# A hybrid decoder layer on one NeuronCore: the MLP's down projection in seven products, with the mixed weight blocks made on GpSimd

## The chip, the core and the metric

The kernel runs on one core of one Trainium2 chip. A core has five engines that work side by side, each with an instruction queue of its own that it takes strictly in order: TensorE (PE in the profile; PEld is its weight load), VectorE (DVE), ScalarE (ACT), GpSimd (POOL) and SyncE (SP), which here issues the weight loads. The metric is the device time of one execution in microseconds.

## The reference

One decoder layer on 512 tokens of 1024 features, all in float32: a mixer with three branches, a cross-attention over 256 memory tokens, and an MLP, each with a norm before it and a residual sum after it, and a last norm. The part that matters here is the MLP:

```python
def squared_relu_mlp(h, w_up, w_down):
    return jnp.square(jax.nn.relu(h @ w_up)) @ w_down        # h: 512 x 1024, w_up: 1024 x 4096, w_down: 4096 x 1024
...
h = rmsnorm(x, norm_mlp_g[l])
x = x + squared_relu_mlp(h, w_up[l], w_down[l])
return rmsnorm(x, final_g)
```

## The kernel before

**Products in three parts.** TensorE takes fp32r operands, so every float32 operand is split into a rounded high part and a low part (ACT casts the high one, DVE subtracts it from the source for the low one), and each product is three matmuls: high by high, high by low, low by high. `parts_of` does this for weights (L111 cast on ACT, L112 subtraction on DVE; both read SBUF), `split` for activations (L223, L224).

**Weights.** `Stream` holds all weight chunks (128 x 1024, 512 KB each) in the order of the plan. `load` issues their DMAs on SP into `w_raw` buffers (RAWS of them); `pump` turns loaded chunks into `w_part` tiles (WBUFS of them, a high and a low tile for each block of 1024 columns) up to AHEAD = 2 steps further than the item that is being issued needs.

**Seven products in place of eight.** A product of two matrices that are each cut into 2 x 2 blocks needs seven block products if sums of the blocks are multiplied (A11 B11, S1 T1, S2 T2, A12 B21, S3 T3, S4 B22, A22 T4; the S are mixes of activation blocks, the T of weight blocks). Six of the gate projections and twelve pairs of the up projection's output blocks are done so by `seven`, with 84 matmuls of 256 columns each (L290). Below, such a group is called a seven. `Seven` makes its weights from two loaded chunks in four steps, s0 (B11), s1 (T1 and T3), s2 (T2 and T4) and s3 (B22 and B21), which fill seven `w_part` tiles; the mixes are made by `combo`, four DVE subtractions of 512 columns into two `w_mix` buffers (L136, L137).

**The MLP.** Four rounds of 1024 hidden features. In round 0 `first_up` makes the eight blocks of 128 features by plain products, in rounds 1 to 3 four sevens make them (q0 to q3 below). After each block comes ReLU and square on ACT and a split into `u_h` and `u_l`. Then comes the down projection of that round by `items_m` and `proj_m`: plain, with the tokens as the stationary operand, 2 column halves x 4 token tiles x 8 blocks x 3 = 192 matmuls of 512 columns, added to `x` by DVE (L836). The last half of the last round runs token tile by token tile, and `final` norms and stores each tile as it is done.

**Order.** The source gives a plan of items. The tile framework's scheduler then sets the order of the instructions on each engine when the program is built, and that order is fixed on the chip; it may move a matmul of one item between those of another.

Of the kernel before, what the change touches and what calls it, by code (L numbers as in the profile page):

```python
# [15 lines left out]
P = 128  # L16
# [16 lines left out]
UNITS, SCRS = 30, 9  # L33
RAWS, WBUFS, AHEAD = 3, 11, 2
# [4 lines left out]
def trunk_kernel(ctx: ExitStack, tc: tile.TileContext, x, mem, par, rot, dqd, kdec, g_mix, g_xa, g_mem, g_mlp,  # L39
# [40 lines left out]


# [43 lines left out]

    class Seven:

# [31 lines left out]

    class Stream:  # L160
        def __init__(self, entries):
            self.loads = [l for e in entries for l in e.loads]
            self.steps, first = [], 0
            for e in entries:
                e.first = first
                for i, st in enumerate(e.steps):
                    self.steps.append((e, st, first + (len(e.loads) if i else 1)))
# [35 lines left out]
    def run_plan():  # L203
        entries, index = [], {}
        for chunks, _ in plan:
            for kind, t, c in chunks:
                k = (t.tensor.name, c)
# [5 lines left out]
        for chunks, fn in plan:  # L213
            es = [index[(t.tensor.name, c)] for _, t, c in chunks]
# [33 lines left out]
    class Mixes:  # L248
# [27 lines left out]
        def __getitem__(self, n):  # L276
# [3 lines left out]
            return [[p[:, t0:t0 + 256] for p in self.a(k0 + k)] for k in range(4)]  # L280

    def seven(b, a):

# [10 lines left out]
        s, u, y1, y2 = scr("sv_s"), scr("sv_u"), scr("sv_1"), scr("sv_2")  # L294
# [8 lines left out]
        dve.tensor_tensor(out=y1[:, lo], in0=p2[:, lo], in1=s[:, lo], op=ALU.add)  # L303
        prod(p1, "S3", "T3", False)
        act.copy(out=u[:, hi], in_=p1[:, lo])
        dve.tensor_tensor(out=y2[:, hi], in0=s[:, hi], in1=u[:, hi], op=ALU.add)
        prod(p3, "S4", "B22", False)
        dve.tensor_tensor(out=y2[:, lo], in0=p3[:, lo], in1=u[:, lo], op=ALU.add)
        prod(p1, "A22", "T4", False)
        return y1, p1, y2  # L310
# [40 lines left out]
    def sumsq(src, c, ss, dst):  # L351

        cs = slice(c * 512, (c + 1) * 512)
        act.activation(out=dst[:, cs], in_=src[:, cs], func=AF.Square, accum_out=ss[:, c:c + 1])
# [7 lines left out]
    def norm_begin(key, src):  # L362
# [4 lines left out]
        sumsq(src, 0, ss, S["xn", key])  # L367
# [3 lines left out]
    def norm_end(key, src, g_bc):  # L371

        xn, ss = S["xn", key], S.pop(("ss", key))
        sumsq(src, 1, ss, xn)
# [593 lines left out]
    def up_done(d):  # L968
        def fn(ps):
            if d == 0:  # L970
                S["u"] = Split("u", KT)
# [179 lines left out]
```

## Time and profile before

| | |
|---|---|
| time, median of 3 runs | 1033.77 us (1033.75 to 1033.93) |
| the profiled execution | 1033.71 us; its span from first to last instruction 1032.0 us |
| PE, matmuls | 1015.5 us busy, 98% |
| DVE | 648.8 us, 63% |
| ACT | 500.7 us, 49% |
| POOL | 66.2 us, 6% |
| weight loads on SP | 27.7% of 16 DMA engines |
| mean granted TensorE clock | 0.999 |

PE's busy time counts matmuls that overlap, since one is issued while the one before still drains; how long a matmul holds PE is read from the distance between starts. The gate sevens run from about 380 to 480 us, round 0 of the MLP from about 690 to 770 us, and rounds 1 to 3 from there to the end.

### The profile page before, as it was taken

The numbers are of one execution on the slowest core, as the hardware profiler recorded it, in microseconds if no ns is written. First come the engines' busy times: TensorE is split into PE (matmuls) and PEld (weight loads), VectorE is DVE, ScalarE is ACT, GpSimd is POOL, SyncE is SP. The second block draws the span as 40 slices with busy tenths as digits, with TensorE's granted clock in tenths as the row PEclk, the third lists the DMA queues.
The fourth block names the chain that finished last, engine by engine and source line by source line (L and its number), as shares of the span: only waits on it lengthen the run. The fifth ranks groups of instructions, "written<-read, shape, count | busy, mean of one in ns | idle before, by whom it ended". The sixth has DMA issues, their size and how long they took to land.

```text
span 1032.0 us, 14325 instructions
## 1 busy us (share of the span) xinstructions
PE 1015.5 (98%) x5636; PEld 884.9 (86%) x5636; DVE 648.8 (63%) x992; ACT 500.7 (49%) x887; POOL 66.2 (6%) x118
## 2 busy tenths in 40 slices
PE   6999999999999999999999999999999999999997
PEld 4888888888888889998898888898889989989985
DVE  5567777856563796784584555466947566565643
ACT  6465567766532154463463444345416624643741
POOL 1101112321110000000100000000000000000000
PEclk9999999999999999999999999999999999999999
DMA  6322233213122212335354213223222321332222
GB/s 265 103 102 81 83 104 102 82 42 123 62 87 79 100 62 83 103 119 198 133 184 163 82 47 118 81 83 123 86 79 82 125 92 71 124 123 80 103 85 81
DMA packets 29876, 106.33 MB, mean 103 GB/s; under 512 B 3569, under 2 KB 3569, under 8 KB 29809
## 3 DMA queue, kind: packets, MB, share of 16 engines
q1 hardware_dynamic: 27216, 98.05, 27.7%
q10 hardware_dynamic: 2592, 7.37, 2.0%
q8 instruction: 44, 0.72, 0.3%
q14 instruction: 24, 0.19, 0.1%
HBM read 103.31 MB, written 2.10 MB: 102 GB/s over the span
## 4 chain that ended last, share of the span: by engine, by line
PE 97%; DMA 1%; DVE 0%; ACT 0%; SPq 0%; issue 0%; DVEq 0%; POOLq 0%; POOL 0%
PE mm L235 24%; PE mm L234 24%; PE mm L236 24%; PE p L290 17%; PE at L385 1%; PE o L546 1%; PE aT L512 1%; DMA w_raw<-in_w_in_dram 1%; PE z L488 1%; PE z L489 0%; PE xsc L236 0%; PE xsc L235 0%; PE xsc L234 0%; PE ro L693 0%; PE sc L667 0%; PE xpp L929 0%
## 5 line engine op out<-in xcount | busy, mean ns | idle before, releaser
L112 DVE TENSOR_TENSOR w_part<-w_raw,w_part 128x1024 fp32r<-128x1024 f32 (+1 forms) x180 | 210.9, 1176 | 168.1 <-PE mm L235 75.2
L111 ACT CAST w_part<-w_raw 128x1024 fp32r<-128x1024 f32 (+1 forms) x180 | 180.6, 1006 | 135.2 <-PE mm L236 79.1
L234 PE MATMUL mm<-hT_h,w_part 128*128 128x512 f32 (+1 forms) x512 | 193.6, 379 | 0.0
L235 PE MATMUL mm<-hT_l,w_part 128*128 128x512 f32 (+1 forms) x512 | 193.3, 378 | 0.0
L236 PE MATMUL mm<-hT_h,w_part 128*128 128x512 f32 (+1 forms) x512 | 193.0, 378 | 0.0
L290 PE MATMUL p<-mix_h,w_part 128*128 128x256 f32 x576 | 112.2, 283 | 0.5 <-ACT sv_s L297 0.5
L236 PEld LDWEIGHTS mm<-hT_h,w_part 128*128 128x128 f32 x512 | 96.4, 188 | 17.1
L234 PEld LDWEIGHTS mm<-hT_h,w_part 128*128 128x128 f32 x512 | 96.2, 188 | 16.8
L235 PEld LDWEIGHTS mm<-hT_l,w_part 128*128 128x128 f32 x512 | 96.5, 188 | 16.4
L235 PE MATMUL mm<-w_part,u_h 128*128 128x512 f32 x256 | 99.8, 390 | 0.0
L234 PE MATMUL mm<-w_part,u_h 128*128 128x512 f32 x256 | 98.6, 390 | 0.0
L236 PE MATMUL mm<-w_part,u_l 128*128 128x512 f32 x256 | 98.2, 389 | 0.0
L290 PEld LDWEIGHTS p<-mix_h,w_part 128*128 128x128 f32 x576 | 93.4, 192 | 1.4 <-ACT sv_s L297 0.7
L290 PE MATMUL p<-hT_h,w_part 128*128 128x256 f32 x432 | 84.4, 283 | 0.0
L290 PE MATMUL p<-mix_l,w_part 128*128 128x256 f32 x288 | 81.5, 283 | 0.0
L290 PEld LDWEIGHTS p<-hT_h,w_part 128*128 128x128 f32 x432 | 70.1, 192 | 0.8
L111 ACT CAST w_part<-w_mix 128x1024 fp32r<-128x1024 f32 x36 | 37.8, 1051 | 55.9 <-PE mm L235 37.5
L112 DVE TENSOR_TENSOR w_part<-w_mix,w_part 128x1024 fp32r<-128x1024 f32 x36 | 44.0, 1221 | 26.7 <-ACT w_part L111 20.0
L290 PE MATMUL p<-hT_l,w_part 128*128 128x256 f32 x216 | 60.7, 283 | 0.0
L236 PEld LDWEIGHTS mm<-w_part,u_l 128*128 128x128 f32 x256 | 48.1, 188 | 9.8
L235 PEld LDWEIGHTS mm<-w_part,u_h 128*128 128x128 f32 x256 | 48.1, 188 | 9.5
L234 PEld LDWEIGHTS mm<-w_part,u_h 128*128 128x128 f32 x256 | 47.9, 188 | 9.5
(211 smaller groups left out, 1813.2 us busy)
## 6 DMA issues: line engine op xcount, KB each, us to landing
w_raw<-in_w_in_dram SPq DMA_DIRECT2D x52, 512.0 KB, 3.4
w_raw<-in_w_up_dram SPq DMA_DIRECT2D x32, 512.0 KB, 3.6
w_raw<-in_w_down_dram SPq DMA_DIRECT2D x32, 512.0 KB, 3.4
w_raw<-in_w_br_dram SPq DMA_DIRECT2D x12, 512.0 KB, 3.4
w_raw<-in_w_gate_dram SPq DMA_DIRECT2D x12, 512.0 KB, 3.5
w_raw<-in_w_o_dram SPq DMA_DIRECT2D x8, 512.0 KB, 3.5
w_raw<-in_w_xk_dram SPq DMA_DIRECT2D x8, 512.0 KB, 4.2
w_raw<-in_w_xv_dram SPq DMA_DIRECT2D x8, 512.0 KB, 3.5
```

Of the source, the lines that this page charges most:

```text
L111: act.copy(out=wh, in_=src)
L112: dve.tensor_tensor(out=wl, in0=src, in1=wh.bitcast(F32), op=ALU.subtract)
L234: te.matmul(ps, lh, rh, start=first, stop=False)
L235: te.matmul(ps, lh, rl, start=False, stop=False)
L236: te.matmul(ps, ll, rh, start=False, stop=last)
L290: te.matmul(ps[:, :256], x[:, k, :], y, start=first and k == 0 and i == 0, stop=k == 3 and i == 2, skip_group_check=True)
L385: te.transpose(ps[:, k * P:(k + 1) * P], xn[:, c * P:(c + 1) * P], ident)
L488: te.matmul(z[:, :s], q[:, e, tsl], S["skh", hp][:, e, :s], start=True, stop=False)
L512: te.transpose(aps[:, sb * P:(sb + 1) * P], a[:, sb * P:(sb + 1) * P], ident)
L546: te.matmul(dst, vv, rhs, start=sb == 0 and i == 0, stop=sb == nblk and i == 1, skip_group_check=True)
```

## The change

The down projection of each round is done as seven block products as well, with the tokens as the stationary operand: for each of the seven (P1 to P7, in `ORDER`) two token tiles x 4 blocks x 3 = 24 matmuls of 512 columns, 168 a round. `_pack_d` lays the same eight chunks out by blocks: two each of B11, B12, B22, B21. `Wide` makes two blocks of 1024 columns for each product, j = 0 and 1; four of the seven (P5, P6, P7, P4) are differences of chunks and are made on GpSimd by `minus`, in place in the loaded buffers. `Seven` does its mixes with `minus` on GpSimd in place too, so that `combo` and the `w_mix` buffers go. The activations of each round are now kept as blocks: `u_ready` makes, from the squared values `s` and `u` of a pair, two sums and differences `u_v` and `u_w` in four GpSimd instructions of 256 columns, and splits `s`, `u_v`, `u_w` and half of `u` into `u_a`, `u_s`, `u_t` and `u_b`. `first_up`'s blocks 4 to 7 are done in two halves of 256 tokens. Buffers: RAWS 3 to 6, WBUFS 11 to 8, UNITS 30 to 32. The norm's statistics start from the other column half.

```diff
-UNITS, SCRS = 30, 9
-RAWS, WBUFS, AHEAD = 3, 11, 2
+UNITS, SCRS = 32, 9
+RAWS, WBUFS, AHEAD = 6, 8, 2
...
+    def minus(out, a, b):
+        pool.tensor_tensor(out=out, in0=a, in1=b, op=ALU.subtract)
...
-        def combo(self, a0, a1, b0, b1):
-            x = wpool.tile([P, CW], F32, name="w_mix", bufs=2)
-            dve.tensor_tensor(out=x[:, :512], in0=a0, in1=a1, op=ALU.subtract)
-            dve.tensor_tensor(out=x[:, 512:], in0=b0, in1=x[:, :512] if b1 is None else b1, op=ALU.subtract)
-            return x
...
         def s1(self, raw):
-            ra, rb = raw
-            self.x1 = self.combo(ra[:, 512:], ra[:, :512], rb[:, :512], ra[:, 512:])
-            return parts_of(self.x1)
+            l, r = raw[0][:, :512], raw[0][:, 512:]
+            minus(l, r, l)
+            minus(r, raw[1][:, :512], r)
+            return parts_of(raw[0])
         def s2(self, raw):
-            rb = raw[1]
-            return parts_of(self.combo(rb[:, :512], self.x1[:, :512], rb[:, 512:], None))
+            l, r = raw[0][:, :512], raw[0][:, 512:]
+            minus(l, raw[1][:, :512], l)
+            minus(r, raw[1][:, 512:], l)
+            return parts_of(raw[0])
...
+    ORDER = ("P1", "P5", "P6", "P7", "P3", "P2", "P4")
+    class Wide:
...
+            t = r["B11", j]
+            if self.p == "P1":
+                src = t
+            elif self.p == "P5":
+                minus(t, r["B12", j], t)
+                src = t
+            elif self.p == "P6":
+                minus(t, r["B22", j], t)
+                src = t
+            elif self.p == "P7":
+                src = r["B12", j]
+                minus(src, r["B22", j], src)
+            elif self.p == "P4":
+                minus(t, r["B21", j], t)
+                src = t
+            else:
+                src = r[dict(P3="B22", P2="B21")[self.p], j]
+            return parts_of(src)
...
+    def u_ready(q, s, u):
+        act.activation(out=s, in_=s, func=AF.Square)
+        act.activation(out=u, in_=u, func=AF.Square)
...
+        v, w = scr("u_v"), scr("u_w")
+        pool.tensor_tensor(out=v[:, LH], in0=u[:, RH_], in1=s[:, RH_], op=ALU.add)
+        minus(v[:, RH_], s[:, LH], u[:, RH_])
+        put("u_a", s)
+        minus(w[:, LH], v[:, LH], s[:, LH])
+        put("u_s", v)
+        minus(w[:, RH_], u[:, LH], w[:, LH])
+        hi, lo = u_parts("u_b", 0)
+        split(hi[:, q, :], lo[:, q, :], u[:, LH])
+        put("u_t", w)
...
-    for r in range(4):
-        up7(r)
-        items_m(w_down, 8 * r, lambda: S["u"], add_x(0))
-        if r < 3:
-            items_m(w_down, 8 * r + 4, lambda: S["u"], add_x(1))
...
+    LEFT = dict(P1="A11", P5="S1", P6="S2", P7="S3", P3="S4", P2="A12", P4="A22")
+    def down(r):
...
+                    for kk in range(4):
+                        ah, al = [x[:, tok] for x in u_block(LEFT[p], kk)]
+                        bh, bl = [x[:, (kk % 2) * 512:(kk % 2) * 512 + 512] for x in ws[kk // 2]]
+                        for n, (x, y) in enumerate(((ah, bh), (ah, bl), (al, bh))):
+                            te.matmul(ps, x, y, start=p in ("P1", "P5", "P2") and kk == 0 and n == 0,
+                                      stop=kk == 3 and n == 2, skip_group_check=True)
+                    t, c = TO[p]
+                    dst = S["x"][t + i][:, c * 512:(c + 1) * 512]
+                    dve.tensor_tensor(out=dst, in0=ps, in1=dst, op=ALU.add)
```

The lines move: the weight cast and subtraction are L127 and L128 in the changed kernel, the activation split L281 and L282, `minus` L143, the sevens' matmuls L349 and their copies and sums L356 to L366, the new down matmuls L1147.

**Place 1: ACT, round 2 of the MLP, around the end of seven q0.** The sevens write the PSUM tiles p1_7746 (q0) and p1_7888 (q1) before and p1_7901 and p1_8046 now. Before, w_part_7866 and w_part_7870 are the high parts of q1's s2 and s3.

```order
L297 COPY sv_s_7749<-p1_7746 128x256
L111 CAST w_part_7728<-w_raw_7627 128x1024
L111 CAST w_part_7736<-w_raw_7657 128x512
L111 CAST w_part_7742<-w_mix_7739 128x1024
L111 CAST w_part_7866<-w_mix_7863 128x1024
L299 COPY sv_s_7749<-p3_7748 128x256
L301 COPY sv_u_7750<-p1_7746 128x256
L111 CAST w_part_7870<-w_raw_7732 128x1024
```

Now w_part_8025 and w_part_8029 are the high parts of q1's s2 and s3, and L1107 is the ReLU that reads q0's last product:

```order
L360 COPY sv_u_7905<-p1_7901 128x256
L127 CAST w_part_7897<-w_raw_7693 128x1024
L1108 ACTIVATE sv_s_7904<-sv_s_7904 128x512
L1109 ACTIVATE sv_u_7905<-sv_u_7905 128x256
L1045 ACTIVATE sv_s_7904<-sv_s_7904 128x512
L281 CAST u_a_h_8005<-sv_s_7904 128x512
L1107 ACTIVATE sv_u_7905<-p1_7901 128x256
L1046 ACTIVATE sv_u_7905<-sv_u_7905 128x512
L127 CAST w_part_8025<-w_raw_7693 128x1024
L356 COPY sv_s_8049<-p1_8046 128x256
L358 COPY sv_s_8049<-p3_8048 128x256
L127 CAST w_part_8029<-w_raw_7695 128x1024
```

The cast of q1's s2 stood ahead of the copies of q0's second and third products; now it stands behind the ReLU and the square of q0's last.

**Place 2: DVE, the gate sevens, from one item to the next.** mm_3846 before and mm_3839 now are the second branch projection of an item, gt its gate; w_part_3867 before and w_part_3859 now are the low part of the next item's s2.

```order
L303 TENSOR_TENSOR sv_1_3729<-p2_3725,sv_s_3727 128x256
L308 TENSOR_TENSOR sv_2_3730<-p3_3726,sv_u_3728 128x256
L112 TENSOR_TENSOR w_part_3867<-w_mix_3863,w_part_3866 128x1024
L112 TENSOR_TENSOR w_part_3871<-w_raw_3706,w_part_3870 128x1024
L306 TENSOR_TENSOR sv_2_3730<-sv_s_3727,sv_u_3728 128x256
L112 TENSOR_TENSOR w_part_3879<-w_raw_3712,w_part_3878 128x1024
L112 TENSOR_TENSOR w_part_3884<-w_raw_3874,w_part_3884 128x512
L729 TENSOR_TENSOR gt_3844<-mm_3846,gt_3844 128x512
```

Now, with w_part_3716 the low part of the next item's s1:

```order
L787 TENSOR_TENSOR gt_3836<-mm_3839,gt_3836 128x512
L128 TENSOR_TENSOR w_part_3716<-w_raw_3540,w_part_3715 128x1024
L788 TENSOR_TENSOR mg_2563<-mg_2563,gt_3836 128x512
L787 TENSOR_TENSOR gt_3814<-mm_3817,gt_3814 128x512
L788 TENSOR_TENSOR mg_2563<-mg_2563,gt_3814 128x512
L282 TENSOR_TENSOR mgs_3833<-mg_2563,mgs_3832 128x512 x2
L128 TENSOR_TENSOR w_part_3859<-w_raw_3540,w_part_3858 128x1024
```

The next item's s1 and s2 both moved from ahead of the row that waits for the second branch projection to behind it; and s2 is now made by GpSimd in s1's buffer w_raw_3540, so that it starts only when the row of w_part_3716 is done.

**Place 3: POOL, round 2, from seven q3 to the down projection.** Before, GpSimd has no row there. Now w_raw_8033 and 8035 are B11, 8170 and 8172 B12, 8313 and 8315 B22, and u_v_8425 and u_w_8426 belong to q3:

```order
L143 TENSOR_TENSOR w_raw_8033<-w_raw_8170,w_raw_8033 128x1024
L143 TENSOR_TENSOR w_raw_8170<-w_raw_8313,w_raw_8170 128x1024
L143 TENSOR_TENSOR w_raw_8035<-w_raw_8172,w_raw_8035 128x1024
L143 TENSOR_TENSOR w_raw_8033<-w_raw_8313,w_raw_8033 128x1024
L143 TENSOR_TENSOR w_raw_8172<-w_raw_8315,w_raw_8172 128x1024
L143 TENSOR_TENSOR w_raw_8035<-w_raw_8315,w_raw_8035 128x1024
L1053 TENSOR_TENSOR u_v_8425<-sv_u_8329,sv_s_8328 128x256
L143 TENSOR_TENSOR u_v_8425<-sv_s_8328,sv_u_8329 128x256
L143 TENSOR_TENSOR u_w_8426<-u_v_8425,sv_s_8328 128x256
L143 TENSOR_TENSOR u_w_8426<-sv_u_8329,u_w_8426 128x256
```

The mixes of q3's activations stand behind six weight mixes, the last of which overwrites the buffer that P5's second block is split from.

More of the change, by code (lines that the diff above doesn't have):

```diff
@@ L158, in get, with __init__, step @@
                     for n, (i, o) in where.items()}
+    ORDER = ("P1", "P5", "P6", "P7", "P3", "P2", "P4")
+    class Wide:
+        FRESH = dict(P1=0, P5=2, P6=4, P2=6)
+        def __init__(self, t, c):
+            c0, self.p, self.raws = c
+            f = self.FRESH.get(self.p)
+            self.loads = [] if f is None else [(t, c0 + f), (t, c0 + f + 1)]
+            self.steps = [lambda raw, j=j: self.step(raw, j) for j in range(2)]
+            self.parts = []
+        def step(self, raw, j):
+            r = self.raws
+            if self.loads:
+                r[dict(P1="B11", P5="B12", P6="B22", P2="B21")[self.p], j] = raw[j]
+            t = r["B11", j]
[16 more added lines that the diff above has]
+            return parts_of(src)
+        def get(self):
+            return self.parts
     class Stream:
@@ L840, in reload_x, with proj_norm @@
         S["x"] = load_x()
-    def proj_norm(src, a, g, after):
+    def proj_norm(src, a, g, after, parts=lambda: Split("hT", KT)):
         items_m(src, 0, a, add_x(0))
@@ L1122, in _lay_out @@
         "w_up7": _pack_s(a["w_up"][0][:, U7 * P:]),
-        "w_down": np.concatenate([_pack_m(a["w_down"][0, r * D:(r + 1) * D]) for r in range(4)], axis=0),
+        "w_down": _pack_d(a["w_down"][0]),
     }
```

157 lines of the change are left out of this document (101 added, 56 removed).

## The prediction

> **What bounds the kernel now.** I read the shares of busy time, the chain that ended last, and then PE's own list of waits.
>
> ```profile
> PE 1015.5 (98%) x5636; PEld 884.9 (86%) x5636; DVE 648.8 (63%) x992; ACT 500.7 (49%) x887; POOL 66.2 (6%) x118
> ...
> PE 97%; DMA 1%; DVE 0%; ACT 0%; SPq 0%; issue 0%; DVEq 0%; POOLq 0%; POOL 0%
> ...
> PE at L385 <- DVE xn L376: 9.0, 2, 8.5
> PE p L290 <- ACT sv_s L297: 0.5, 1, 0.5
> ```
>
> PE carries 97% of the chain and waited 9.5 us in all, 8.5 of them at the start for the first norm. So the time is the number of matmuls by their distance, and any matmul taken away counts in full, as long as PE is never made to wait. The windows of the stretch that changes show the other engines' room: a stretch that is mostly sevens, and one that is mostly down projection (columns: length, then PE, PEld, DVE, ACT and POOL busy with their counts, clock, DMA).
>
> ```profile
> 843.00:890.00 47.00, 47.00 (x329) 44.18 (x328) 30.30 (x42) 23.54 (x41) 0.00 (x0) 1.00 0.21 74
> 890.00:930.00 40.00, 40.00 (x216) 34.70 (x215) 22.87 (x30) 18.15 (x30) 0.00 (x0) 1.00 0.37 126
> ...
> 843.00:890.00 47.00, 30.85 (x256) 31.02 (x257) 1.00 0.21 74
> ...
> 1016.21 0.39 PE L234 MATMUL mm<-w_part,u_h 128*128 128x512 f32 x1
> ...
> 1024.37 0.39 PE L234 MATMUL mm<-w_part,u_h 128*128 128x512 f32 x1
> ```
>
> The third row is the first window again, L290 alone: 256 matmuls of 256 columns in 30.85 us, 0.1205 us each. Between the last two rows lie 36 matmuls of 512 columns: 8.16 / 36 = 0.227 us each. GpSimd does nothing here before the change.
>
> **The matmuls, term by term.** A round of the down projection goes from 192 matmuls of 512 columns to 168; four rounds take away 96 x 0.227 = 21.8 us. `first_up`'s blocks 4 to 7 go from 96 matmuls of 512 columns to 192 of 256: 192 x 0.1205 - 21.8 = +1.3 us. Without a wait the kernel would take 1033.7 - 20.5 = 1013.2 us (the profiled execution took 1033.71, the median is 1033.77; I count from the former).
>
> **What GpSimd and DVE do to each other.** Before, GpSimd works only in the mixer. Four places where it meets DVE there (start, duration):
>
> ```profile
> 165.98 1.29 POOL L612 TENSOR_TENSOR r_sw<-r_sw,rot 128x512 f32<-128x512 f32 x1
> ...
> 166.05 1.50 DVE L500 TENSOR_TENSOR_SCAN sb_suf<-ones,sb_e 128x128 f32<-128x128 f32 x1 [0.46 <-POOL sb_e L479]
> ...
> 191.99 0.42 DVE L500 TENSOR_TENSOR_SCAN sb_suf<-ones,sb_e 128x128 f32<-128x128 f32 x1 [0.46 <-POOL sb_e L479]
> ...
> 193.47 1.30 POOL L612 TENSOR_TENSOR r_sw<-r_sw,rot 128x512 f32<-128x512 f32 x1 [1.52 <-ACT r_sw L611]
> ...
> 193.42 0.69 DVE L613 TENSOR_TENSOR r_qk<-mm,rot 128x512 f32<-128x512 f32 x1 [0.23 <-ACT r_sw L611]
> 194.15 1.70 DVE L112 TENSOR_TENSOR w_part<-w_raw,w_part 128x1024 fp32r<-128x1024 f32 x1
> ...
> 214.49 1.85 POOL L612 TENSOR_TENSOR r_sw<-r_sw,rot 128x512 f32<-128x512 f32 x1 [1.53 <-ACT r_sw L611]
> ...
> 214.02 1.22 DVE L500 TENSOR_TENSOR_SCAN sb_suf<-ones,sb_e 128x512 f32<-128x512 f32 x1
> ```
>
> A scan that takes 0.42 us took 1.50 beside a GpSimd sum and ended 0.28 us after it; L112 took 1.70 in place of 1.23, ending 1.08 us after the GpSimd sum (194.77); and the GpSimd sum of 214.49 ended 1.10 us after the scan. So an instruction of GpSimd and one of DVE with two SBUF operands run one after the other, whichever comes second waiting, while L613, whose one operand lies in PSUM, kept its 0.69. All of the weight and activation subtractions (L128, L282) have two SBUF operands; the sums from PSUM have not. I take as held: DVE 1.08 to 1.23 us for 1024 columns, GpSimd 1.10 to 1.29 for 512, and by size 2.2 to 2.6 for 1024 and 0.55 to 0.65 for 256, which no row shows. (The Trainium skill, SBUF — State Buffer, section "SBUF: two separate sides", calls this pair of ports an exclusive lock that the loser waits for through a whole instruction. The rows agree. Were it shared instead, the sevens' term below would be only the 29 us of the instruction order, and the sum 1077 us.)
>
> ```profile
> L675 POOL TENSOR_TENSOR r_qd<-r_qk,dqd x4: 1281/1298/1576, 265.2 to 319.8; 128x512 f32<-128x512 f32 x4
> ...
> L112 DVE TENSOR_TENSOR w_part<-w_raw,w_part 128x1024 fp32r<-128x1024 f32 x162 | 199.2, 1230 | 163.9 <-PE mm L235 75.2 <-issue 41.3 <-ACT w_part L111 18.9
> L224 DVE TENSOR_TENSOR u_l<-relu,u_h 128x512 fp32r<-128x512 f32 x32 | 21.8, 686 | 4.4 <-ACT u_h L223 4.4
> L729 DVE TENSOR_TENSOR gt<-mm,gt 128x512 f32<-128x512 f32 x16 | 11.0, 685 | 3.8 <-PE mm L236 3.1 <-ACT gt L773 0.7
> ...
> L111 ACT CAST w_part<-w_raw 128x1024 fp32r<-128x1024 f32 x162 | 169.6, 1049 | 108.7 <-PE mm L236 62.2 <-PE p L290 25.8 <-DMA w_raw<-in_w_in_dram 7.9
> L1011 ACT ACTIVATE relu<-relu 128x512 f32<-128x512 f32 x24 | 15.2, 638 | 0.2
> L1010 ACT ACTIVATE relu<-p 128x256 f32<-128x256 f32 x12 | 4.6, 387 | 4.3 <-PE p L290 4.1
> ```
>
> **The MLP's twelve sevens.** A seven holds PE for 84 x 0.1205 = 10.1 us. The pair of ports is held by GpSimd for four mixes (4.4 to 5.2) and four instructions of `u_ready` (2.2 to 2.6), and by DVE for the weights, 0.54 to 0.69 + 3 x 1.08 to 1.23 (3.8 to 4.4), and for the activations' low parts, three of 512 columns and one of 256 (1.9 to 2.5): 12.3 to 14.7 us. The ports, not PE, bound a seven, by 2.2 to 4.6 us. A second count goes by the order on ACT (first place shown above): q1's third product needs s2, whose cast now stands behind q0's last ReLU and square, 0.39 + 0.64 + 1.05 and then DVE's 1.23 = 3.3 us after q0's last matmul, while PE has 10 matmuls, 1.2 us, to do: 2.1 us of wait. The next block needs s3, behind it on ACT and DVE, and the one after q2's s0: about 1 us more. For q2 and q3 PE comes straight from the last matmul to a product that needs s3 (0.39 + 1.05 + 1.23 = 2.7). So some 3.2 us for three sevens in each round, 9 x 3.2 = 29 us, before any wait at the ports. Both hold at once; I take the middle of the port count, 3.4 x 12 = 41 us, and keep 26 to 55. That WBUFS falls to 8, one more than a seven fills, is why the weights can't be made a whole seven ahead as before.
>
> **The gate sevens.** Six items of 10.1 + 24 x 0.227 = 15.5 us of PE; the ports are held less than that (4.4 to 5.2, 3.8 to 4.4, one plain chunk 1.1 to 1.2, sums and splits up to 2.7: at most 13.5). But by the second place, after the second branch projection come, one behind the other, L787 0.69, s1's L128 1.23, two GpSimd mixes 2.6, s2's cast 1.05 and L128 1.23: 6.8 us, against three products or 4.3 us on PE: 2.5 us of wait, and about 0.9 more for s3, cast next. Five passages from item to item: 17 us, with 0 to 20 as ends (at 0 the sums before it run ahead).
>
> **From q3 to the down projection.** P5's second block gets its `w_part` tiles only when q3's last matmul frees them: 1.05 + 1.23 + signals = 2.4 us in which PE has nothing, and 1.1 us at P5's first block for the same reason. Behind it on POOL (third place) stand P6's second mix and q3's activations, on which P6's and P5's last matmuls wait: up to 2.5 us more. 3.5 to 6 us in each of three rounds, I take 5; in round 0, where plain products leave more time, 0 to 3, I take 2: 17 us. In the rest of a round, the ports hold 14 x 1.08 to 1.23 + 8 x 2.2 to 2.6, at most 38 us with the waits spread, in 168 x 0.227 = 38.1: covered, with no room. DMAs are the same 180 loads, and RAWS = 6 starts them sooner; nothing. Where a stage needs four chunks at once they now fill all eight `w_part` tiles, so the next stage's first weights come later by a cast and a subtraction: 0 to 5 us over four places, I take 1. ACT gains 24 weight casts and 24 splits, DVE loses 72 mixes: inside the counts above. The end, norm and store of the last tiles, stays as it is.
>
> Sum: 1033.7 - 21.8 + 1.3 + 41 + 17 + 17 + 1 = 1089 us. With the low ends (26, 0, 10, 0) 1049, with the high ones (55, 20, 21, 5) 1114.
>
> **The rivals.**
> - *PE is not kept waiting* (faster). The mixes for q0 and q1 are queued on GpSimd ahead of the down projection's end, and DVE is freed of 72 mixes of 0.69 us; if the late casts and the ports' queue were absorbed, 1013 us would come out. It decides where the waits sum to less than 20.5 us, 1.0 us for each of the 21 places (12 sevens, 5 passages, 4 transitions). Against it: the port count alone gives 26. Its near edge, 1032 to 1036, is no measurable change.
> - *Only part of the waits*: the ports' low ends without the order's, PE stalling 23 to 36 us: 1036 to 1049 us.
> - *The clock falls in the waits.* After the long wait at the start PE ran slow, after a short one it did not:
>
> ```profile
> 8.47 1.94 PE L385 MATMUL at<-ident,xn 128*128 128x128 f32 x8 [8.47 <-DVE xn L376]
> 10.53 0.79 PE L234 MATMUL mm<-w_part,hT_h 128*128 128x512 f32 x1
> ...
> 16.26 0.39 PE L234 MATMUL mm<-w_part,hT_h 128*128 128x512 f32 x1
> ...
> 18.55 1.10 PE L385 MATMUL at<-ident,xn 128*128 128x128 f32 x8 [0.51 <-DVE xn L376]
> ```
>
>   The 13 matmuls from 10.53 to 16.26 took 5.7 us in place of 13 x 0.227 = 3.0. If waits between 0.5 and 8.5 us do this, up to 21 times 2.8 us, the time is 1114 to 1148. (The Trainium skill, TensorE: Matmul & The Clock Gate, "What's actually happening", says that the clock halves after an idle window of about 3.4 us; by that my pieces of 1 to 3 us would seldom do it. No run here shows the point.)
>
> **How the numbers follow.** Main case 1049 to 1114 us, 0.68, likeliest 1089. Faster 0.10, same 0.02, part of the waits 0.10, clock 0.10. Leaving out the faster and the unchanged cases (0.12) and the upper part of the clock case (0.06), the range is 1036 to 1122. A change of under 0.2%, 2 us, can't be told from none: faster 0.10, same 0.02, slower 0.88.
>
> **What would show it.** After: PE waits in its list for L128 and ACT's L127, some 75 us in all, where there were 9.5; the distance of wide matmuls still 0.227; L143 at 1.3 us for 512 columns alone but with a mean well above it, and L128 above 1.23, each stretched by the other; rounds 1 to 3 at 95 to 100 us each. I am wrong if L128 keeps its 1.23 us beside GpSimd, if ACT's late casts are met by a PE that is late itself, or if PE's waits stay under 20 us.

## The result and the profile after

The changed kernel takes 1124.36 us (median of four runs, 1123.5 to 1125.5) against 1033.81 for the kernel before: 1.088 times as long, 95% interval 1.086 to 1.090. The prediction said slower, 1089 us, 1036 to 1122: the side was right, the time 35 us off and 2 us outside the range.

Shares of busy time, then the chain that ended last by engine, on the page of the changed kernel (profiled execution 1125.5 us, span 1123.8):

```profile
PE 1041.1 (93%) x5636; PEld 896.9 (80%) x5636; DVE 738.2 (66%) x984; ACT 541.6 (48%) x939; POOL 333.0 (30%) x286
...
PE 11%; DVE 7%; POOL 6%; ACT 3%; issue 3%; POOLq 0%; DVEq 0%
```

PE was on 97% of the chain before, and is on 11% now; DVE and GpSimd stand on it beside PE. PE is idle for 1123.8 - 1041.1 = 82.7 us, where it was idle for 16.5: 66 us more. But it is also *busy* for 1041 us, with work that should take about 995 (1015.5 less the 20.5 saved). The second 46 us are not waits, and one look at the granted clock says most of what they are. Mean clock of the kernel before and, below it, of the changed one:

```profile
core 0: 1032.0 us, clock 0.999
```

```profile
core 0: 1123.8 us, clock 0.966
```

The clock of this trace is 1.0 or 0.5, never between; its records put 75.4 us of the span at half clock. PE was idle for 12.2 us of these (summed over the pieces), so it lost half of 63: 32 us. Waits 66 and clock 32 on top of the 1011.5 us that the span would have without them (1032.0 less 20.5) make 1109.5; the last 14 us I can account for only in part: the profile counts the whole of a matmul that follows a wait as busy, 0.28 or 0.39 us where the next comes after 0.12 or 0.23, so each of some 50 waits hides another 0.16 us, 8 in all.

PE's own waits, longest sums first (total, times, longest):

```profile
PE p L349 <- ACT w_part L127: 17.7, 15, 2.2
PE p L349 <- DVE w_part L128: 13.7, 14, 2.2
PE at L443 <- DVE xn L434: 9.8, 3, 8.5
PE p L1147 <- ACT u_s_h L281: 8.3, 1, 8.3
PE p L1147 <- DVE u_a_l L282: 7.4, 4, 2.0
```

The third row is the old start. The first two are the weights that the prediction named, 31 us of them in the sevens. The single wait of 8.3 us is new and stands in round 0. The stretching that the prediction named is there too, from 380 us on:

```profile
L128 DVE TENSOR_TENSOR w_part<-w_raw,w_part 128x1024 fp32r<-128x1024 f32 x163 | 231.3, 1430 | 110.6 <-ACT w_part L127 110.2
...
L143 POOL TENSOR_TENSOR w_raw<-w_raw 128x512 f32<-128x512 f32 x69 | 96.3, 1396 | 151.7 <-DVE w_part L128 149.2
...
L282 DVE TENSOR_TENSOR u_a_l<-sv_s,u_a_h 128x512 fp32r<-128x512 f32 x16 | 22.9, 1430 | 13.7 <-ACT u_a_h L281 13.7
```

DVE's subtraction for the weights took 1.23 us on average before and takes 1.43 now, that for the activations 0.69 and now 1.43; a GpSimd mix of 512 columns averages 1.40 us, where the shortest took 1.28.

The windows of round 0's down projection and of rounds 1 and 2, each from the first matmul of one to the first of the next:

```profile
751.71:808.85 57.14, 42.12 (x171) 33.34 (x170) 50.68 (x55) 22.02 (x32) 24.84 (x15) 0.88 0.22 74
808.85:911.53 102.68, 90.42 (x505) 78.64 (x504) 73.24 (x72) 50.57 (x78) 63.57 (x41) 0.92 0.25 82
911.53:1013.69 102.16, 88.08 (x506) 75.97 (x505) 73.33 (x72) 50.58 (x78) 63.56 (x41) 0.95 0.25 83
```

Round 0 holds 38.1 us of matmuls in 57.1 us; a whole round holds 78.6 (4 x 84 x 0.1205 + 38.1) in 102.

### The profile page after: what moved, and what is told of

It is laid out like the page before. It is cut to its first block, busy times and chain, and to the rows that moved or that the text cites. A ratio compares the mean times of both kernels' runs of the same rounds, so it can differ in the third digit from the quotient of the medians.

```text
span 1123.8 us, 14661 instructions
## 1 busy us (share of the span) xinstructions
PE 1041.1 (93%) x5636; PEld 896.9 (80%) x5636; DVE 738.2 (66%) x984; ACT 541.6 (48%) x939; POOL 333.0 (30%) x286
## 5 line engine op out<-in xcount | busy, mean ns | idle before, releaser
L128 DVE TENSOR_TENSOR w_part<-w_raw,w_part 128x1024 fp32r<-128x1024 f32 (+1 forms) x240 | 317.4, 1332 | 165.4 <-ACT w_part L127 161.8
L127 ACT CAST w_part<-w_raw 128x1024 fp32r<-128x1024 f32 (+1 forms) x240 | 242.3, 1016 | 276.0 <-PE mm L293 119.2
L143 POOL TENSOR_TENSOR w_raw<-w_raw 128x512 f32<-128x512 f32 (+1 forms) x104 | 195.6, 1886 | 204.5 <-DVE w_part L128 179.5
L349 PE MATMUL p<-mix_h,w_part 128*128 128x256 f32 x576 | 125.5, 305 | 20.3 <-ACT w_part L127 8.7
L349 PEld LDWEIGHTS p<-mix_h,w_part 128*128 128x128 f32 x576 | 102.2, 209 | 25.1 <-ACT w_part L127 10.1
L294 PEld LDWEIGHTS mm<-hT_h,w_part 128*128 128x128 f32 x544 | 102.8, 189 | 15.7
L292 PEld LDWEIGHTS mm<-hT_h,w_part 128*128 128x128 f32 x544 | 102.6, 189 | 15.1
L349 PE MATMUL p<-hT_h,w_part 128*128 128x256 f32 x432 | 94.2, 301 | 17.8 <-ACT w_part L127 8.9
L349 PEld LDWEIGHTS p<-hT_h,w_part 128*128 128x128 f32 x432 | 76.0, 204 | 22.8 <-ACT w_part L127 18.4
L349 PE MATMUL p<-mix_l,w_part 128*128 128x256 f32 x288 | 86.3, 300 | 0.0
L349 PE MATMUL p<-hT_l,w_part 128*128 128x256 f32 x216 | 64.3, 298 | 0.0
L349 PEld LDWEIGHTS p<-mix_l,w_part 128*128 128x128 f32 x288 | 60.5, 210 | 0.4
L1147 PE MATMUL p<-w_part,u_s_h 128*128 128x512 f32 x128 | 45.4, 440 | 12.4 <-ACT u_s_h L281 8.3
L1147 PE MATMUL p<-w_part,u_t_h 128*128 128x512 f32 x128 | 42.0, 402 | 4.8 <-DVE x L1151 2.7
L349 PEld LDWEIGHTS p<-hT_l,w_part 128*128 128x128 f32 x216 | 44.7, 207 | 0.5
L1147 PE MATMUL p<-w_part,u_a_h 128*128 128x512 f32 x128 | 42.7, 413 | 2.2 <-ACT u_a_h L281 2.1
```

Source lines behind the costliest of these rows:

```text
L127: act.copy(out=wh, in_=src)
L128: dve.tensor_tensor(out=wl, in0=src, in1=wh.bitcast(F32), op=ALU.subtract)
L143: pool.tensor_tensor(out=out, in0=a, in1=b, op=ALU.subtract)
L292: te.matmul(ps, lh, rh, start=first, stop=False)
L294: te.matmul(ps, ll, rh, start=False, stop=last)
L349: te.matmul(ps[:, :256], x[:, k, :], y, start=first and k == 0 and i == 0, stop=k == 3 and i == 2, skip_group_check=True)
```

## Where the clock goes down

The first matmuls after the wait in the third gate item, on PE's timeline:

```profile
420.56 0.42 PE L349 MATMUL p<-hT_l,w_part 128*128 128x256 f32 x1
420.78 0.42 PE L349 MATMUL p<-mix_h,w_part 128*128 128x256 f32 x1
420.99 0.42 PE L349 MATMUL p<-mix_l,w_part 128*128 128x256 f32 x1
```

They come 0.215 us apart, where matmuls of 256 columns come 0.12 apart elsewhere. The windows of three pieces of 3.41 us in a row around this place, then of one pair in the next item (length, PE busy and count, ..., granted clock third from the end):

```profile
416.92:420.34 3.42, 0.80 (x5) 0.40 (x3) 1.19 (x2) 2.51 (x4) 1.25 (x1) 1.00 0.00 0
420.34:423.75 3.41, 3.41 (x15) 3.33 (x16) 2.43 (x3) 0.97 (x2) 0.00 (x0) 0.50 0.55 180
423.75:427.16 3.41, 3.41 (x27) 3.27 (x26) 0.42 (x1) 0.71 (x2) 0.00 (x0) 1.00 0.80 279
437.41:440.82 3.41, 0.87 (x5) 0.67 (x6) 3.41 (x4) 3.18 (x5) 0.96 (x1) 1.00 0.00 0
440.82:444.23 3.41, 3.41 (x17) 3.22 (x16) 2.16 (x2) 0.90 (x2) 0.00 (x0) 0.50 0.59 190
```

A piece in which PE is idle for 2.6 us is followed by one at half clock, 3.41 us long, and then the clock is full again. The borders lie on one fixed grid through the whole run (420.34, 440.82, 461.30, 481.78, all whole numbers of 3.413 us apart), whatever PE does. I went through the pieces of all 19 traces (from 60 us on, those that came behind two at full clock): each of the 125 slow ones stands behind a piece with at least 1.27 us of idle, and behind more than 1.92 us not one stayed at full clock. Between 1.3 and 1.9 both occur. So it isn't the length of one wait that counts but the idle share of a piece, and the same wait can fall across a border and cost nothing. In e13_scr below, a gate passage with the same 2.6 us of idle shows it, split 1.4 and 1.2 over two pieces; the next passage, not split, pays:

```profile
414.97:418.38 3.41, 1.97 (x17) 1.76 (x15) 1.86 (x3) 1.11 (x3) 2.94 (x2) 1.00 0.00 0
418.38:421.80 3.42, 2.24 (x16) 2.04 (x17) 2.71 (x3) 2.59 (x3) 0.00 (x0) 1.00 0.09 18
421.80:425.21 3.41, 3.41 (x27) 3.24 (x26) 1.21 (x2) 0.88 (x2) 0.00 (x0) 1.00 0.85 315
435.45:438.87 3.42, 0.78 (x5) 0.42 (x4) 3.42 (x4) 3.06 (x5) 1.22 (x1) 1.00 0.00 0
438.87:442.28 3.41, 3.41 (x16) 3.31 (x17) 2.41 (x3) 1.04 (x2) 0.00 (x0) 0.51 0.56 186
```

(The Trainium skill, TensorE: Matmul & The Clock Gate, "What's actually happening", has the free-running window of 3413 ns, and these runs agree to the digit. It speaks of an idle window; here a window that was a little over half idle was enough.) The expectations below name the gates' slow pieces as 431 to 496 us; they lie at 420 to 485, since the clock's records have a zero of their own, 11.3 us before the first instruction, which I had missed. e9's "summed over about 7 us" came of the same slip.

## The experiments

Medians beside runs of the kernel before (1033.7 to 1033.9 throughout), if not said otherwise. "Round 2" is from its first seven to the next round's.

| run | what differs | us | ratio, 95% | round 2 | clock |
|---|---|---|---|---|---|
| changed kernel | | 1124.4 | 1.086 to 1.090 | 102.2 | 0.966 |
| e2_nomix_seven | no mixes of the sevens | 1087.5 | 1.050 to 1.054 | 95.5 | 0.984 |
| e6_nomix_both | nor of the down projection | 1042.8 | 1.007 to 1.010 | 84.8 | 0.995 |
| e3_apart | sevens' mixes in tiles of their own | 1101.9 | 1.064 to 1.068 | 102.0 | 0.976 |
| e5_all_dve | all mixes on DVE | 1076.5 | 1.039 to 1.042 | 92.2 | 0.986 |
| e8_wide_dve | down projection's mixes on DVE | 1105.5 | 1.067 to 1.071 | 98.5 | 0.975 |
| e14_w10 | ten w_part tiles | 1111.0 | 1.073 to 1.076 | 103.5 | 0.964 |
| e15_dve_w10 | on DVE, ten tiles | 1066.6 | 1.030 to 1.033 | 90.8 | 0.984 |
| e16_dve_apart | on DVE, tiles of their own | 1061.0 | 1.025 to 1.028 | 90.8 | 0.990 |
| e4_bufs | kernel before, the new buffers | 1044.7 | 1.009 to 1.012 | 87.5 | 0.999 |

**What the mixes cost, taken away.** e2 leaves out the `minus` calls of `Seven`, e6 those of `Wide` too; what comes out is then no product of these weights, and only the time is of use. e2 leaves out 72 mixes, e6 all 104 of the weights; the 64 instructions of `u_ready` stay on GpSimd in both.

```diff
-            minus(l, r, l)
-            minus(r, raw[1][:, :512], r)
...
-            minus(l, raw[1][:, :512], l)
-            minus(r, raw[1][:, 512:], l)
```

> The changed kernel without the four GpSimd subtractions of each seven's weights (72 in all are left out, the chunks go in unmixed). Both the theory of the ports and that of the chain in place put the sevens' waits on these: PE's waits at the sevens (about 40 us of the 82.7 idle) go to under 10, the clock's pieces from 21 to under 9: 1124 - 35 - 20 = 1070 us, 1060 to 1080. Theory 'eight w_part tiles and late casts': waits stay with the mixes gone, 1110 to 1124 us.

> The changed kernel without the mixes of the sevens' weights and of the down projection's (104 less the 48 of u_ready and its sums are left out; chunks go in unmixed). Theory 'ports', with P5, P6 and P7 one behind the other needing 2 x 2.4 us of GpSimd and 3.7 of DVE each against 5.4 of PE: the waits in the down projection go, a round takes 80 to 86 us in place of 95 without the sevens' mixes alone, 1040 to 1055 us. Theory 'eight w_part tiles in the down projection': the waits for L128 there stay, 1075 to 1087 us.

e2 went 37 us down, not 54: 1087.5. The gates came back to 15.55 us an item, but PE's list then has one new first row, in the down projection:

```profile
PE p L1143 <- DVE w_part L128: 23.5, 16, 2.8
```

The waits that the sevens' mixes made go, and the down projection's own come forward. With those mixes out too, 1042.8 us, as the ports' theory had it; so the weights' mixes carry 82 of the 91 us, each kind about half (37 and 45). The eight `w_part` tiles, which stay, don't make the down projection wait by themselves.

**Where the mixes are written.**

```diff
-UNITS, SCRS = 32, 9
+UNITS, SCRS = 30, 9
...
-            minus(l, r, l)
-            minus(r, raw[1][:, :512], r)
-            return parts_of(raw[0])
+            ra, rb = raw
+            x = self.x = wpool.tile([P, CW], F32, name="w_mix", bufs=2)
+            minus(x[:, :512], ra[:, 512:], ra[:, :512])
+            minus(x[:, 512:], rb[:, :512], ra[:, 512:])
+            return parts_of(x)
...
```

> The changed kernel with the sevens' mixes still on GpSimd, but written to two tiles of their own (w_mix, two buffers, paid for with two of the 32 units) and not over the loaded chunk, so that s2's mix no longer waits until s1's cast and subtraction have read the chunk. Theory 'chain in place' (s1's subtraction, then two mixes of 1.3 to 1.45, then s2's cast, one behind the other): the wait at the third product goes as it does without the mixes, 1070 to 1085 us. Theory 'ports' (GpSimd and DVE hold the pair for longer than a seven of PE): the MLP's sevens stay at 14 to 16 us, only the gates gain, 1100 to 1120 us.

1101.9 us, in the ports' range. The windows of two gate items, 15.53 and 16.64 us long where they took 20.2 (in the profiled execution, which took 1109.3 us):

```profile
412.27:427.80 15.53, 15.53 (x109) 14.55 (x108) 11.38 (x14) 8.10 (x13) 6.04 (x5) 1.00 0.30 102
427.80:444.44 16.64, 15.82 (x110) 14.62 (x109) 11.60 (x14) 8.37 (x14) 4.70 (x4) 1.00 0.29 95
```

In the gates it was the chain in place, as far as it ran too late; in the MLP a round stays at 102 us, as the ports' theory said. GpSimd's own pace, 1.28 us for a mix of 512 columns where DVE takes 0.69, is in the same count, and this run does not tell the two apart.

**Which engine mixes.**

```diff
     def minus(out, a, b):
-        pool.tensor_tensor(out=out, in0=a, in1=b, op=ALU.subtract)
+        dve.tensor_tensor(out=out, in0=a, in1=b, op=ALU.subtract)
...
-        pool.tensor_tensor(out=v[:, LH], in0=u[:, RH_], in1=s[:, RH_], op=ALU.add)
+        dve.tensor_tensor(out=v[:, LH], in0=u[:, RH_], in1=s[:, RH_], op=ALU.add)
```

> The changed kernel with every mix (sevens', down projection's, u_ready's) on DVE in place of GpSimd, same order, still over the loaded chunk. Theory 'ports': the pair is held 0.69 us for 512 columns and 1.23 for 1024 in place of 1.3 and 2.4, so a round of the MLP has some 81 us of DVE against 78.4 of PE and takes 85 to 90 us in place of 102; the gate items come from 20.2 to about 17; with the pieces of slow clock that go, 1050 to 1070 us. Theory 'DVE has no room for more': a round stays at 100 or grows, 1115 to 1140 us.

> The changed kernel with the down projection's mixes alone (8 of 1024 columns in a round) on DVE. Theory 'ports': 8 x (2.4 - 1.23) = 9 us less held in a round, just where P5 to P7 wait: 4 x 9 = 36 us, with the clock up to 45: 1078 to 1095 us. Theory 'DVE bounds the down projection itself': 1110 to 1130 us.

With all mixes on DVE (e5) the engine that already had the most work beside PE took over what kept GpSimd busy for 267 us (333.0 less the mixer's 66.2), and the kernel became 48 us faster, 1076.5, 6 us above the ports' range; a round is 92 us, 2 above what I gave it. This takes away two things at once, the exclusion and GpSimd's slower pace; how the 48 us divide between them is not shown. Moving the down projection's mixes alone (e8) gave 19 us, half of what the ports' theory said: PE then waits for DVE's sums instead (PE p L1147 <- DVE x L1151: 12.7 us, longest 6.1). I take it, though no run shows it, that DVE still meets the sevens' and the activations' mixes on GpSimd, with more of its own to do.

**The buffers.**

```diff
-RAWS, WBUFS, AHEAD = 3, 11, 2
+RAWS, WBUFS, AHEAD = 6, 8, 2
```

That is e4, in the kernel before. e14 and e15 have ten `w_part` tiles, for two units less; e16 keeps eight, and writes the sevens' mixes to tiles of their own as e3 does.

> The kernel before with the changed kernel's buffers alone: RAWS 6 in place of 3, WBUFS 8 in place of 11; mixes on DVE in w_mix, plain down projection. Theory 'ports' or 'chain in place': the buffers cost next to nothing, 1034 to 1040 us. Theory 'late casts, since weights can't be made a seven ahead': about 2 us in each of the 12 MLP sevens and 1 to 2.5 in the gates, plus the clock, 1055 to 1080 us.

> The changed kernel with ten w_part tiles in place of eight, paid for with two units. Theory 'the low number of w_part tiles carries some 11 us, as in the kernel before with these buffers': 1106 to 1115 us. Theory 'in the changed kernel the ports are behind the same waits, so more tiles help no more': 1118 to 1126 us.

> Every mix on DVE and ten w_part tiles. If exclusion and tiles are separate causes, 1076 - 11 = 1060 to 1068 us; if DVE's own work is what is left, 1072 to 1078 us. To be under the kernel before's 1034 the waits would have to fall to under 20 us, which neither theory gives.

> Every mix on DVE, the sevens' into two tiles of their own. The chain in place on DVE is two mixes of 0.69, a cast and a subtraction; it left 0.95 us in a gate passage. Theory 'chain in place': the gates come to 15.6 us and the MLP's sevens lose 1 us each, 1058 to 1068 us. Theory 'DVE's order': 1072 to 1080 us.

In the kernel before, the buffers alone cost 10.9 us, between my two theories; in the MLP PE waits for casts that now come late, and nowhere else:

```profile
PE p L290 <- ACT w_part L111: 6.8, 9, 1.0
```

Two more tiles in the changed kernel give 13.4 us back (e14), and 10 where all mixes are on DVE (e15). The range for e14 was met by luck: the theory put the loss in the MLP, as in e4, and the gain lies in the gates. With the mixes still on GpSimd and still in place, the items run without a wait, since s2's cast starts 2.4 us before its item and no longer 4.1 us behind its start; the six items take 94.6 us in place of 113.5, and what comes after them is some 4.5 us longer.

```profile
412.49:428.05 15.56, 15.56 (x110) 14.56 (x109) 8.75 (x13) 7.65 (x13) 5.55 (x4) 1.00 0.31 102
```

So in the gates the chain in place costs time only where the tiles are missing: curing either is nearly enough (0.8 us of idle left in e3, none in e14). e16, with every mix on DVE and the sevens' in tiles of their own, is the best of the variants at 1061.0 us, still 2.6% above the kernel before. No run here points to a version that beats the kernel before: with the weights' mixes left out altogether (e6), a round of 84.8 us is no shorter than the 84.0 before.

**Round 0.**

```diff
-            plan.extend(mix[i:i + 1])
-        plan.extend(mix[U7 - n:])
+        S["late"] = mix
...
+            if r == 0:
+                plan.extend([S["late"].pop(0)] if S["late"] else [])
...
```

> The changed kernel with the mixes of the tokens (DVE L319 and L323, two SBUF operands, some 32 instructions of 0.68 us and their splits) put behind the products P1, P5 and P6 of round 0 in place of first_up's last blocks. Theory 'round 0 is held by DVE's token mixes, which shut GpSimd out of u_ready' (u_v waited 5.7 us for a buffer and took 4.05 us): the wait of 8.3 us and the four slow pieces there go, round 0 from 57 us to 42 to 47: 1109 to 1114 us. Theory 'the work is only moved': the same waits stand later in round 0, 1120 to 1130 us.

1123.2 us: the work was only moved. The wait of 8.3 us went, but others took its place: the longest in round 0 is now 4.6 us, behind DVE's sum into `x`, and PE is idle for 2.1 and 1.6 us more in rounds 1 and 2.

```diff
-UNITS, SCRS = 32, 9
+UNITS, SCRS = 31, 11
```

> The changed kernel with 11 scratch tiles in place of 9 (SCRS), paid for with one unit (31 in place of 32). In round 0 GpSimd's first sum of u_ready stood 5.7 us behind DVE L282, which freed the scratch tile that it writes. Theory 'round 0 waits for a scratch tile': the wait of 8.3 us and its slow pieces go, round 0 from 57 us to 44 to 48, 1110 to 1116 us. Theory 'round 0 waits for the ports, DVE being busy 19.7 of 20 us': 1119 to 1126 us.

1136.0 us, outside both; why it is 12 us longer, with one unit fewer, I did not follow up. PE's wait of 8.3 us stays as it was, so two more scratch tiles don't cure it. They don't clear the scratch tile either: GpSimd's sum still stands 4.04 us behind a cast of the token mixes, where it stood 5.71 before, although the values that it adds were ready 14 us earlier. What comes after that wait, the time at the ports, this timeline shows better than the changed kernel's own. GpSimd's first sum of `u_ready` for the last pair of blocks of round 0, 256 columns, and the instruction that follows it:

```profile
766.84 6.32 POOL L1053 TENSOR_TENSOR u_v<-sv_u,sv_s 128x256 f32<-128x256 f32 x1 [4.04 <-ACT mix_h L281]
773.12 0.72 POOL L143 TENSOR_TENSOR u_v<-sv_s,sv_u 128x256 f32<-128x256 f32 x1
```

and DVE in the same time:

```profile
766.62 1.21 DVE L128 TENSOR_TENSOR w_part<-w_raw,w_part 128x1024 fp32r<-128x1024 f32 x1
767.75 0.68 DVE L319 TENSOR_TENSOR mix<-hT_h,hT_l 128x512 f32<-128x512 f32 x1
768.35 2.48 DVE L282 TENSOR_TENSOR mix_l<-mix,mix_h 128x512 fp32r<-128x512 f32 x4
770.76 0.68 DVE L323 TENSOR_TENSOR mix<-mix 128x512 f32<-128x512 f32 x1
771.36 1.21 DVE L128 TENSOR_TENSOR w_part<-w_raw,w_part 128x1024 fp32r<-128x1024 f32 x1
772.50 1.27 DVE L1151 TENSOR_TENSOR x<-p,x 128x512 f32<-128x512 f32 x2
```

DVE has eight instructions with two SBUF operands one behind the other, and GpSimd's sum, 0.7 us of work, is held up until they are through. It ends 0.66 us after DVE turns to L1151, whose one operand lies in PSUM. In the changed kernel the same sum takes 4.05 us, DVE's run ends at 773.70, and the sum 0.67 us later:

```profile
770.32 4.05 POOL L1053 TENSOR_TENSOR u_v<-sv_u,sv_s 128x256 f32<-128x256 f32 x1 [5.71 <-DVE mix_l L282]
```

```profile
773.10 0.68 DVE L282 TENSOR_TENSOR mix_l<-mix,mix_h 128x512 fp32r<-128x512 f32 x1
773.70 1.28 DVE L1151 TENSOR_TENSOR x<-p,x 128x512 f32<-128x512 f32 x2
```

and PE waits for what is cut from it:

```profile
775.76 2.08 PE L1147 MATMUL p<-w_part,u_s_h 128*128 128x512 f32 x4 [8.27 <-ACT u_s_h L281]
```

**The ports by themselves.** The kernel before, with work on GpSimd that nobody waits for but the chunk's release; one run each.

```diff
+            for _ in range(8):
+                pool.tensor_tensor(out=side, in0=ra[:, :256], in1=ra[:, 256:512], op=ALU.subtract)
```

and with `pool.tensor_copy(out=side, in_=ra[:, :256])` in its place.

> The kernel before with eight GpSimd subtractions of 256 columns in each seven (two SBUF operands, from the loaded chunk into a tile that nobody reads), which nothing waits for but the chunk's release. Theory 'ports': GpSimd's instruction and DVE's with two SBUF operands go one after the other, so L112's mean rises from 1.23 to above 1.4 in the sevens' stretches, each stretched one by a GpSimd instruction of some 0.65, while sums from PSUM keep 0.69; the time 1034 to 1045 us. Theory 'no exclusion, GpSimd is only slow by itself': L112 stays at 1.23 us and the time at 1033 to 1036.

> The same with eight GpSimd copies of 256 columns (one SBUF operand) in place of the subtractions. Theory 'only two operands on both sides exclude': L112 at 1.23 us as in the kernel before, time 1033 to 1036 us. Theory 'GpSimd's access alone shuts DVE out': L112 stretched as with the subtractions.

The groups of the gates' stretch in the kernel before, then with the subtractions (1045.7 us), then with the copies (1034.0 us):

```profile
L112 DVE TENSOR_TENSOR w_part<-w_mix,w_part 128x1024 fp32r<-128x1024 f32 x10 | 12.2, 1220 | 1.2 <-ACT w_part L111 1.2
...
L729 DVE TENSOR_TENSOR gt<-mm,gt 128x512 f32<-128x512 f32 x13 | 8.9, 685 | 3.8 <-PE mm L236 3.1 <-ACT gt L773 0.7
...
L306 DVE TENSOR_TENSOR sv<-sv_s,sv_u 128x256 f32<-128x256 f32 x6 | 2.5, 418 | 0.0
```

```profile
L148 POOL TENSOR_TENSOR side<-w_raw 128x256 f32<-128x256 f32 x38 | 50.8, 1338 | 21.7 <-DMA w_raw<-in_w_gate_dram 19.1
L113 DVE TENSOR_TENSOR w_part<-w_mix,w_part 128x1024 fp32r<-128x1024 f32 x10 | 13.1, 1306 | 0.0
...
L732 DVE TENSOR_TENSOR gt<-mm,gt 128x512 f32<-128x512 f32 x13 | 8.8, 680 | 2.3 <-ACT gt L776 2.3
L309 DVE TENSOR_TENSOR sv<-sv_s,sv_u 128x256 f32<-128x256 f32 x6 | 4.6, 774 | 0.0
```

```profile
L148 POOL COPY side<-w_raw 128x256 f32<-128x256 f32 x32 | 22.4, 699 | 52.4 <-DMA w_raw<-in_w_gate_dram 50.7
...
L113 DVE TENSOR_TENSOR w_part<-w_mix,w_part 128x1024 fp32r<-128x1024 f32 x10 | 12.7, 1272 | 0.6 <-ACT w_part L112 0.5
...
L309 DVE TENSOR_TENSOR sv<-sv_s,sv_u 128x256 f32<-128x256 f32 x6 | 3.1, 517 | 0.0
```

The subtraction on GpSimd is stretched to twice the copy's time (1338 against 699 ns; one of 256 columns took 0.72 us beside DVE's L1151, above), DVE's sum of two SBUF operands, L306 and then L309, from 418 ns to 774, and the product that reads PSUM, L729 and then L732, not at all (685 and 680). The weights' subtraction rose only from 1.22 to 1.31 us, less than the 1.4 that I expected: DVE lost less by this than GpSimd did. With the copies DVE is stretched a little too, the sum to 517 ns and the weights' subtraction to 1.27 us, where I had expected 1.23, so one operand on GpSimd's side isn't free of it; the kernel's time stayed.

**The clock by itself.**

```diff
         prod(p3, "S1", "T1", True)
+        for _ in range(16):
+            te.matmul(p3[:, :256], nul[:, :P], nul, start=False, stop=True, skip_group_check=True)
```

> The changed kernel with 16 matmuls of 256 columns that add zero, put behind the second product of each of the 18 sevens, where PE waits for the third product's weights; 16 x 0.1205 = 1.93 us each. Theory 'idle share sets the clock': of the 21 pieces of 3.41 us at clock 0.5, the four in the gates and about nine behind the MLP's sevens go, 13 x 1.7 = 22 us less, and the filling costs some 7 us where the wait is shorter than 1.93 us (the first two gate items, the first seven of a round): 1105 to 1112 us, with the stretch 380 to 500 at clock 1.00. Theory 'the clock falls for another reason, the other engines' work': the clocks stay, the filling takes the place of the waits: 1124 to 1135 us.

> The changed kernel with 16 zero matmuls (1.93 us) behind the second product of the third to sixth gate item alone, where PE waits 2.6 us. Theory 'idle time of PE halves the clock': these four items come from 20.2 to about 18.7 us and the four slow pieces of 431 to 496 us go, 1124 - 4 x 1.5 = 1117 to 1120 us, although PE does 7.7 us more. Theory 'the slow pieces have another cause': the four items stay at 20.2, 1123 to 1126 us.

Filling in every seven (e1) gave 1137.4 us, outside what I expected of either: in the gates it did what it should (clock 1.00 from 380 to 500 us), in the MLP PE only waited later, in the down projection. Filling the third to sixth gate item alone (e17; five rounds) settles it: 1119.0 us, ratio 1.081 to 1.084, 5.3 us faster than the changed kernel with 7.7 us more work on PE. One of the four items, 18.8 us long in place of 20.2, at clock 1.00:

```profile
414.03:432.82 18.79, 18.04 (x126) 16.65 (x125) 9.46 (x13) 7.54 (x12) 5.86 (x4) 1.00 0.25 85
```

The other engines do the same work there as before, so it is PE's own idleness, and not their work, that the clock answers to here.

To find from which wait on, I added waits to the kernel before, with a chain of four ACT instructions in e9 (shown) and of seven in e10 (one run each):

```diff
+        act.mul(out=nul, in_=p3[:, :256], mul=0.0)
+        for _ in range(3):
+            act.mul(out=nul, in_=nul.bitcast(F32), mul=0.0)
+        te.matmul(p1[:, :256], nul[:, :P], nul, start=False, stop=True, skip_group_check=True)
```

> The kernel before, with one wait of PE made on purpose in each of its 18 sevens: behind the second product a chain of four ACT instructions of 256 columns multiplies its result by zero, and one matmul that adds this zero must come before the third product: some 1.0 to 1.5 us idle each time. Theory 'it is the idle time summed over about 7 us that halves the clock, from some 2.5 us on' (from the changed kernel's gates: 2.62 us of idle in a passage was followed by 3.41 us at 0.5 each time, 0.95 us in the gates with all mixes on DVE never): no slow piece, 1034 + 18 x 1.4 = 1055 to 1062 us. Theory 'any wait of over a microsecond does it': 18 slow pieces, 1085 to 1092 us.

> The same with a chain of seven, so some 1.9 to 2.3 us idle each time. Theory 'from some 2.5 us in about 7 us on': still no slow piece, or only where a wait is above 2.5, 1034 + 18 x 2.3 = 1072 to 1080 us. Theory 'from 1.5 to 2 us on': about one slow piece for each seven, 1095 to 1110 us.

1040.4 and 1053.3 us. These missed what they were for: other matmuls came to lie in the gap, and PE's waits on the chain were no longer than 0.6 and 0.8 us; none of those was followed by a slow piece. In e10 two longer waits for weights came up, and one, with 1.98 us idle in one piece, has its slow piece:

```profile
924.29:927.70 3.41, 1.43 (x6) 1.10 (x7) 2.31 (x3) 2.43 (x4) 0.00 (x0) 1.00 0.55 192
927.70:931.12 3.42, 3.42 (x14) 2.93 (x13) 3.22 (x6) 0.00 (x0) 0.00 (x0) 0.50 0.54 175
```

## Why the prediction was off, step by step

- *The matmuls, -21.8 and +1.3.* The page counts 5636 matmuls as before, which is what 96 and 96 fewer and 192 more make, and in the gates of e14, where nothing waits, an item takes the 15.5 us that the prediction gave it. No run has the down projection without waits, so its 21.8 us are not shown by themselves.
- *The ports.* Right as a mechanism (e11 against e12, and L128 and L282 in the changed kernel), and wrong in one clause: that the one that comes second waits for *the other's instruction*. GpSimd waited through eight of DVE's (e13). (The Trainium skill, SBUF — State Buffer, "SBUF: two separate sides", says that whoever starts first keeps the pair for its whole instruction; that alone doesn't give the 6.32 us, since DVE also took it again each time.) The sum of held times gave 41 us of wait for twelve sevens plus 15 for three down projections, 18.7 a round; PE's idle time in rounds 1 and 2 was 12.3 and 14.1, so the count was too high by a third or more.
- *The gate sevens, +17.* The place was right, the waits a third shorter: the six items hold 11.3 us of idle. Four slow pieces, 13.7 us, half of it lost, came on top, so the stretch took 113.5 us where it takes 94.6 without a wait (e14), 19 more. The term is near this by luck, since the two errors go against each other. That the missing tiles were behind it (e14) I had not seen.
- *Round 0, +2, between 0 and 3.* The first of the two steps that failed, a term taken far too small. I had counted on the "plain products" there to leave time, and had not looked at what DVE does in them: the token mixes, all with two SBUF operands. The stage lost 19 us, 15 of them idle, the rest mostly clock. How much of its longest wait is the ports and how much the scratch tile that the same mixes hold is open (e13). A look at DVE's shares in the profile before would have told: in its window from 720 to 740 us DVE is busy for 20.0 of 20 us.
- *The w_part tiles, +1.* 10.9 us in the kernel before (e4), 13.4 in the changed one (e14). I had looked only at stages with four chunks at once; the loss is in the MLP's sevens in e4 and in the gates in the changed kernel.
- *The waits in all, 75 us.* 66 measured. Rounds 1 to 3 hold 39 us of new idle time where 56 were forecast, the gates 11 for 17, round 0 15 for 2: two terms too large by 23 in all, one too small by 13.
- *The clock.* The second step that failed, and the one that took the time out of the range. It stood as a rival at 0.10 with "1114 to 1148", and in the sum as nothing; it cost 32 us. The main case and this rival did not exclude each other: whoever forecasts 21 waits of 2 to 5 us has to price them at the clock's rate too. The rows before bounded the point between 0.5 and 8.5 us, and I took the upper side without a row that showed it. With 32 us, 1089 would have been 1121.
- *Rivals.* PE kept busy (1013): no; even without any mix of weights 1042.8. Part of the waits (1036 to 1049): no.

## What to carry to other kernels

A wait on PE costs its length, and where it fills about half of a 3.4 us piece it costs up to 1.7 us more at half clock: filling four waits of 2.6 us with matmuls that add zero made this kernel 5.3 us faster. GpSimd is no free engine beside DVE: before work with two SBUF operands goes there, count how long DVE's runs of such work are, and not how busy GpSimd is; the same work on DVE was 48 us cheaper. And when buffers pay for a change, price them by themselves: here they alone cost the kernel before 10.9 us.

## What the runs showed of the hardware that I had not expected

- The clock falls by pieces of 3.413 us on a fixed grid, and right behind a piece in which PE was idle for about 1.3 to 1.9 us or more. What decides between these two numbers stays open; the share of the array's work in the rest of the piece may count, and was not tried.
- A GpSimd instruction of 0.7 us took 6.32 us behind a run of eight DVE instructions, and got through when DVE turned to an operand in PSUM. The other way round, beside GpSimd subtractions of 256 columns DVE lost less: a mean of 1.31 us where 1.22 was due; beside the changed kernel's longer mixes it was 1.43 for 1.23.
- A GpSimd copy, with one SBUF operand, beside the same DVE work ran at 0.70 us for 256 columns and cost the kernel nothing (1034.0 us), though DVE's short sums rose from 418 to 517 ns and its weights' subtraction from 1.22 to 1.27 us.
